# Nearest-neighbour upsampling: 512 consecutive rows per partition, larger DMA descriptors, loads on a second queue

## The chip, the cores and the metric

The kernel runs on one core of a Trainium2 chip. The metric is device time in microseconds (us). A time quoted below is the median of a kernel's runs. "Span" is the length of one profiled execution; it is 1.8 us shorter than the time of that same run (for the kernel before, the record does not say which run was profiled).

## The reference

Every element of a float32 array of shape (16, 64, 64, 64) is repeated twice in both image directions. Nothing is computed.

```python
for i in range(new_h):          # 128
    for j in range(new_w):      # 128
        result[:, :, i, j] = x[:, :, i // 2, j // 2]
```

A core has 16 DMA engines, which move data between HBM (the large memory outside the core) and SBUF (the core's own memory, 128 partitions). A descriptor moves one contiguous run of bytes, and the trace shows it as one packet. The input has 65,536 rows of 64 floats (256 bytes each, 16.8 MB). Each input row becomes two equal output rows of 512 bytes, which lie next to each other in HBM (67.1 MB in all).

## The kernel before

A tile gives each of the 128 partitions K = 32 consecutive input rows. One tile of output is therefore one contiguous stretch of 4 MiB, and neighbouring partitions are 32 KiB apart in it. VectorE expands the first half of the rows, ScalarE the second half: four strided copies each. All loads are issued first, on SyncE's DMA queue, into eight buffers that hold the whole input. The 16 stores follow on the same queue, from two u buffers.

```python
K = 32; rows = P * K; J = 2
# group = 8, which is all of the input
for ti in range(ti0, ti0 + group):
    xt = xpool.tile([P, J, K, W], fdt, name="xt")
    # ... (the first tile comes as two loads of 1 MiB)
    src = src.rearrange("(j p k) w -> p j (k w)", j=J, p=P)   # 8 KiB runs
    nc.sync.dma_start(out=xt[:, :, :, :], in_=src)
for t in range(ti0 * J, (ti0 + group) * J):
    u2 = upool.tile([P, K, s, W, s], fdt, name="u2")          # two buffers
    # ... rows 0..15 on VectorE, 16..31 on ScalarE, for each hd and wd:
    #     copy u2[:, lo:hi, hd, :, wd] <- xt[:, j, lo:hi, :]
    nc.sync.dma_start(out=of[r0 : r0 + rows, :], in_=u2[:, :, :, :, :])  # 32 KiB runs
```

## Time and profile before

| | before |
|---|---|
| time | 200.81 us (200.73 to 201.08, 3 runs) |
| span | 199.2 us |
| VectorE / ScalarE busy | 20% / 34% |
| packets of the 16 DMA engines | 98.5% of the span |
| longest part of the chain | stores, 67% |

These lines are from the page of the kernel before. The rows DMA and GB/s cut the span into 40 slices: the busy share in tenths, and what was moved. The line q1 is the DMA queue table: packets, MB, and the time of its packets as a share of 16 engines' span. The last two lines are the chain of work that ended last, by engine and by line.

```profile
span 199.2 us, 246 instructions
...
DVE 40.0 (20%) x64; ACT 68.0 (34%) x65; POOL 0.2 (0%) x4
...
DMA  6999999999999999999999999999999999999995
GB/s 214 423 438 421 423 421 424 421 500 421 421 421 421 421 421 441 480 447 421 421 421 421 421 421 461 474 428 428 421 421 421 424 421 467 461 421 421 428 428 217
...
q1 hardware_dynamic: 4496, 83.89, 98.5%
...
DMA 69%; ACT 18%; SPq 3%; ACTq 1%; issue 0%
DMA out_dram<-u 67%; ACT u L88 18%; SPq L90 3%; DMA xt<-in_x_dram 2%; ACTq L121 1%; ACTq L88 0%
```

The DMA engines have no hole from the second slice to the second last. The 18% of ScalarE on the chain are not a bottleneck: those copies run while the other u buffer is being stored. The timeline shows it, here at three steady tiles (start, duration, engine, what, and in brackets the idle time before and what ended it).

```profile
101.10 4.18 ACT L88 COPY u<-xt 128x1024 f32<-128x1024 f32 x4 [5.54 <-DMA out_dram<-u]
...
110.80 4.18 ACT L88 COPY u<-xt 128x1024 f32<-128x1024 f32 x4 [5.53 <-DMA out_dram<-u]
...
120.51 4.16 ACT L88 COPY u<-xt 128x1024 f32<-128x1024 f32 x4 [5.52 <-DMA out_dram<-u]
```

One tile takes 9.7 us, of which ScalarE idles 5.5. The trace also records every packet. A 32 KiB store packet takes 1.213 us, nearly without exception, and eight of them on an engine are the 9.7 us of a tile. So the time is the sum of packet times on one engine, plus the start and the tail. Only fewer, shorter or better filled packets can change it.

### The profile page before, as it was taken

What the parts mean: (1) busy time and instruction counts of PE and PEld (TensorE: products, weight loads), DVE (VectorE), ACT (ScalarE), POOL (GpSimd) and SP (SyncE); (2) the same over time, 40 slices, a digit from 0 to 9 for tenths busy, and PEclk for the clock granted to TensorE, in tenths of its full rate; (3) what the DMA queues carried; (4) which work ended last, traced back from release to release, by engine and by line L of the source; (5) the groups of instructions that cost most, each with busy time, mean ns of one, the idle gap of its engine ahead of it and who ended that gap; (6) DMA issues with size and microseconds to landing.
All of it is one profiled execution on the core that took longest, in us unless ns stands there. A gap on an engine that the chain in (4) does not pass through costs nothing.

```text
span 199.2 us, 246 instructions
## 1 busy us (share of the span) xinstructions
DVE 40.0 (20%) x64; ACT 68.0 (34%) x65; POOL 0.2 (0%) x4
## 2 busy tenths in 40 slices
DVE  0810000000404050505050505050505050504000
ACT  2870000000444352626161708080808080808000
POOL 0000000000000000000000000000000000000000
DMA  6999999999999999999999999999999999999995
GB/s 214 423 438 421 423 421 424 421 500 421 421 421 421 421 421 441 480 447 421 421 421 421 421 421 461 474 428 428 421 421 421 424 421 467 461 421 421 428 428 217
DMA packets 4499, 83.90 MB, mean 421 GB/s; under 512 B 401, under 2 KB 401, under 8 KB 401
## 3 DMA queue, kind: packets, MB, share of 16 engines
q1 hardware_dynamic: 4496, 83.89, 98.5%
q14 instruction: 3, 0.02, 0.0%
HBM read 16.78 MB, written 67.11 MB: 421 GB/s over the span
## 4 chain that ended last, share of the span: by engine, by line
DMA 69%; ACT 18%; SPq 3%; ACTq 1%; issue 0%
DMA out_dram<-u 67%; ACT u L88 18%; SPq L90 3%; DMA xt<-in_x_dram 2%; ACTq L121 1%; ACTq L88 0%
## 5 line engine op out<-in xcount | busy, mean ns | idle before, releaser
L88 ACT COPY u<-xt 128x1024 f32<-128x1024 f32 x64 | 66.7, 1136 | 114.6 <-DMA out_dram<-u 111.0
L86 DVE COPY u<-xt 128x1024 f32<-128x1024 f32 x64 | 40.0, 690 | 141.7 <-DMA out_dram<-u 136.1
L88 ACT ACT_TABLE_LOAD x1 | 1.3, 1283 | 0.7 <-PEq L107 0.7
L107 POOL MEMSET const-uint8-127<- 128x1 uint8 x1 | 0.1, 102 | 0.0
L107 POOL MEMSET const-bfloat16-1.0<- 128x1 bf16 x1 | 0.1, 101 | 0.0
L107 POOL MEMSET const-float32-0.0<- 128x1 f32 x1 | 0.1, 99 | 0.2 <-issue 0.2
L107 POOL MEMSET const-float32-1.0<- 128x1 f32 x1 | 0.1, 98 | 0.0
## 6 DMA issues: line engine op xcount, KB each, us to landing
out_dram<-u SPq DMA_DIRECT2D x16, 4096.0 KB, 15.1
xt<-in_x_dram SPq DMA_DIRECT2D x7, 2048.0 KB, 24.4
xt<-in_x_dram SPq DMA_DIRECT2D x2, 1024.0 KB, 5.8
```

The source lines that it names most:

```text
L86: nc.vector.tensor_copy(out=dst, in_=src_ap)
L88: nc.scalar.copy(out=dst, in_=src_ap)
L90: nc.sync.dma_start(out=of[r0 : r0 + rows, :], in_=u2[:, :, :, :, :])
L107: nc = _bacc.Bacc("TRN2", target_bir_lowering=False, num_devices=1)
L121: with _tile.TileContext(nc) as tc:
```

## The change

The intent is larger descriptors. Partition p owns input rows 512p to 512p+511. A load takes 128 of them (32 KiB descriptors where 8 KiB were), a store takes K = 64 (64 KiB where 32 KiB were). Three other things come with it:

- Neighbouring partitions are now 512 KiB apart in the output, and 128 KiB apart in the input.
- Loads are issued by ScalarE, on a second DMA queue. The xt buffers hold half of the input, so two of the four loads are issued between stores.
- VectorE takes 40 of 64 rows.

```diff
-    xf = x.rearrange("b c h w -> (b c h) w")
-    of = out.rearrange("b c (h hd) w -> (b c h) (hd w)", hd=s)
-    K = 32
+    RP = R // P
+    xf = x.rearrange("b c h w -> (b c h) w").rearrange("(p r) w -> p r w", p=P)
+    of = out.rearrange("b c (h hd) w -> (b c h) (hd w)", hd=s).rearrange(
+        "(p r) w -> p r w", p=P
+    )
+    K = 64
     J = 2
+    KV = 40
# ... (xt: 2 buffers of J*K rows; u: 2 buffers)
+    def load(c):
+        xt = xpool.tile([P, J * K, W], fdt, name="xt")
+        nc.scalar.dma_start(
+            out=xt[:, :, :], in_=xf[:, c * J * K : (c + 1) * J * K, :]
+        )
+        xts[c] = xt
+    for c in range(min(2, nloads)):
+        load(c)
+    for t in range(nloads * J):
# ... (copies as before, rows 0..KV on VectorE, KV..K on ScalarE)
-                nc.sync.dma_start(out=of[r0 : r0 + rows, :], in_=u2[:, :, :, :, :])
+        nc.sync.dma_start(
+            out=of[:, t * K : (t + 1) * K, :], in_=u[:, :, :, :, :]
+        )
+        if j == J - 1 and c + 2 < nloads:
+            load(c + 2)
```

More of the change, by code (lines that the diff above doesn't have):

```diff
@@ L14 @@
     x: bass.AP,
-    scale_factor: bass.AP,
+    scale_factor: int,
     out: bass.AP,
@@ L19 @@
     P = nc.NUM_PARTITIONS
-    s = int(scale_factor) if not isinstance(scale_factor, bass.AP) else None
-    assert s is not None and s >= 1
+    s = int(scale_factor)
     B, C, H, W = x.shape
@@ L26 @@
     fdt = x.dtype
-    esz = 4 if fdt == mybir.dt.float32 else mybir.dt.size(fdt)
-    xf = x.rearrange("b c h w -> (b c h) w")
-    of = out.rearrange("b c (h hd) w -> (b c h) (hd w)", hd=s)
-    K = 32
-    while K > 1 and R % (P * K) != 0:
-        K //= 2
-    assert R % (P * K) == 0, f"{R} input rows not tileable into {P} partitions"
-    rows = P * K
-    ntiles = R // rows
-    J = 2
-    while ntiles % J != 0:
-        J //= 2
-    n_in = ntiles // J
-    u2_bytes = K * s * W * s * esz * 2
@@ L44 @@
-    xt_bytes = J * K * W * esz
-    group = max(1, min(n_in, (200 * 1024 - u2_bytes) // xt_bytes))
-    while n_in % group != 0:
-        group -= 1
-    k_dve = (K + 1) // 2
-    with (
-        tc.tile_pool(name="xin", bufs=group) as xpool,
-        tc.tile_pool(name="uexp", bufs=2) as upool,
-    ):
-        for ti0 in range(0, n_in, group):
-            xts = {}
-            for ti in range(ti0, ti0 + group):
-                xt = xpool.tile([P, J, K, W], fdt, name="xt")
-                if ti == 0:
-                    for j in range(J):
-                        nc.sync.dma_start(
-                            out=xt[:, j, :, :],
-                            in_=xf[(ti * J + j) * rows : (ti * J + j + 1) * rows, :],
-                        )
-                else:
-                    src = xf[ti * J * rows : (ti + 1) * J * rows, :]
-                    if J > 1:
-                        src = src.rearrange("(j p k) w -> p j (k w)", j=J, p=P)
-                    nc.sync.dma_start(out=xt[:, :, :, :], in_=src)
-                xts[ti] = xt
-            for t in range(ti0 * J, (ti0 + group) * J):
-                ti, j = divmod(t, J)
-                r0 = t * rows
-                xt = xts[ti]
-                u2 = upool.tile([P, K, s, W, s], fdt, name="u2")
-                for ei, (lo, hi) in enumerate(((0, k_dve), (k_dve, K))):
-                    if lo >= hi:
-                        continue
-                    src_ap = xt[:, j, lo:hi, :]
-                    for hd in range(s):
-                        for wd in range(s):
-                            dst = u2[:, lo:hi, hd, :, wd]
-                            if ei == 0:
-                                nc.vector.tensor_copy(out=dst, in_=src_ap)
-                            else:
-                                nc.scalar.copy(out=dst, in_=src_ap)
-                nc.sync.dma_start(out=of[r0 : r0 + rows, :], in_=u2[:, :, :, :, :])
@@ new lines @@
+    RP = R // P
[4 more added lines that the diff above has]
+    K = 64
+    J = 2
+    nloads = RP // (J * K)
+    assert nloads * J * K == RP
+    KV = 40
+    xpool = ctx.enter_context(tc.tile_pool(name="xin", bufs=2))
+    upool = ctx.enter_context(tc.tile_pool(name="uexp", bufs=2))
+    xts = {}
+    def load(c):
[4 more added lines that the diff above has]
+        xts[c] = xt
@@ new lines @@
+    for c in range(min(2, nloads)):
+        load(c)
+    for t in range(nloads * J):
+        c, j = divmod(t, J)
+        xt = xts[c]
+        u = upool.tile([P, K, s, W, s], fdt, name="u")
+        for lo, hi, copy in ((0, KV, nc.vector.tensor_copy), (KV, K, nc.scalar.copy)):
+            for hd in range(s):
+                for wd in range(s):
+                    copy(
+                        out=u[:, lo:hi, hd, :, wd],
+                        in_=xt[:, j * K + lo : j * K + hi, :],
+                    )
+        nc.sync.dma_start(
+            out=of[:, t * K : (t + 1) * K, :], in_=u[:, :, :, :, :]
+        )
+        if j == J - 1 and c + 2 < nloads:
+            load(c + 2)
```

## The prediction

"The same page" in the text below is "DMA: Bandwidth & Descriptors" of the Trainium skill. Its 214 GB/s, the full rate, was measured at a pitch of 4 MiB padded by 4 KiB.

> **What bounds the kernel now.** The 16 DMA engines. The DMA queue table puts their packets at 98.5% of the 199.2 us span. The slice table shows DMA at 9 in every slice but the first and the last. In the chain of waits, 69% is DMA (67% stores). VectorE (20% busy) and ScalarE (34%) idle mainly for "DMA out_dram<-u" (136 and 111 us). The timeline repeats every 9.71 us, which is exactly eight 32 KiB packets of 1.213 us on each engine.
>
> The packet records add up to it. Each engine moves 128 store packets of 32 KiB, 1.2136 us each: 155.3 us. And 128 load packets of 8 KiB, 0.317 us each: 40.6 us. Together 195.9 us. The remaining 3.3 us are start (first data near 1.7 us) and tail (last packet ends at 198.0 us).
>
> **What the change does.**
> - Load packets go from 8 KiB to 32 KiB. If a 32 KiB read takes what a 32 KiB write takes now, 32 x 1.213 = 38.8 us: saves 1.8 us.
> - Store packets go from 32 to 64 KiB. Fitting the two sizes (0.309 us undisturbed at 8 KiB, 1.213 us at 32 KiB) gives about 8 ns fixed per packet and 27.2 B/ns. So 64 x 2.418 = 154.7 us: saves 0.6 us, or nothing if a 64 KiB run is split in two.
> - Loads move to ScalarE's queue and interleave with the stores, where before all loads came first. I assume that this leaves the total the same.
> - The first load is 4 MiB: it lands near 12.5 us where the first 1 MiB took to 5.5 us. The copies of tile 0 take some 6.5 us, so store 0 issues near 19.5 us. The second load keeps the engines busy until about 22 us: no hole. Afterwards 6.5 us of copies hide behind a 19.4 us store.
> - The VectorE/ScalarE rebalance is off the critical path.
> - If the 1.28 us activation-table load sits before the first load on ScalarE, the start slips by up to 1.3 us.
>
> Balance without any slowdown of the stores: 200.8 - 2.4 + 0 to 1.3 = 198.4 to 199.7 us. All of it is on the critical path, because that is DMA packet time.
>
> **The risk.** Stores now step 512 KiB between partitions (32 KiB before), all engines in step. The same page (Latency and other measured facts, HBM row pitch at large powers of two) gives 207 GB/s per direction at 512 KiB pitch against 214[...], 3% less, for copies between HBM tensors. Here writes run at 432 GB/s, so the effect could be absent or larger. 3% on 155 us is 4.7 us, an estimate from that page: about 203.5 us. I give a visible slowdown of the stores roughly one chance in three.
>
> **Predicted: 200.0 us, 80% range 197.2 to 208.** Faster by over 2%: 0.08; within 2%: 0.62; slower by over 2%: 0.30.
>
> **What would show it.**
> - Right: DMA share still about 98%; 32 KiB reads near 1.21 us; 64 KiB writes near 2.42 us (or 32 KiB pieces at 1.213); no slice below 9 after the first; chain of waits still mainly stores.
> - Pitch at work: store packets longer than 2.42 us, GB/s below 420 in the late slices that hold only stores, while the DMA share stays near 98%.
> - Wrong on overlap: a slice near 20 us, or later, with the DMA share falling, and copies waiting for xt.
>
> **What would make it wrong.** A strong pitch effect on the writes (far over 3%); reads and writes mixed on one engine running better or worse than alone; a hole in the DMA at the first store or at a load that is too late.

## The result, and the profile after

The changed kernel takes 203.61 us (202.75 to 204.12, 4 runs) against 200.86 us of the kernel before beside it. The ratio is 1.0131, 95% interval 1.0102 to 1.016. It is 1.3% slower: inside the 2% that count as the same, but clear of the noise.

These are the same lines of the page of the changed kernel. Queue q1 now carries stores only, and q10 (ScalarE's) the loads.

```profile
span 201.4 us, 147 instructions
...
DVE 45.5 (23%) x32; ACT 50.6 (25%) x33; POOL 0.2 (0%) x4
...
DMA  7999989799999999999998999999999999999990
GB/s 286 443 417 417 521 319 501 312 417 410 527 417 417 430 417 417 443 391 365 430 514 384 430 443 443 456 456 430 417 417 430 417 417 456 430 443 443 469 443 39
...
q1 hardware_dynamic: 1152, 67.11, 77.8%
q10 hardware_dynamic: 576, 16.78, 20.1%
...
DMA 68%; ACT 15%; ACTq 1%; issue 0%
DMA out_dram<-u 62%; ACT u L59 15%; DMA xt<-in_x_dram 6%; ACTq L98 1%; ACTq L59 0%
```

The packets still fill 97.9% of the span (77.8 + 20.1), so the time is still packet time. The last slice has hardly any traffic (39 GB/s where 217 were). The first half has slices on either side of 417 GB/s, while from the 23rd slice to the second last they are about as steady as before. A packet is booked whole where it starts, so single slices swing, in GB/s and in the busy share; read them over several slices. The 8, 7 and 8 in the sixth, eighth and 22nd slice are not holes: worked out from the packets' durations, the engines are busy for all of every stretch of 5 us from 5 to 195 us.

The timeline of the changed kernel shows the start as predicted.

```profile
0.72 0.85 ACTq L45 DMA_DIRECT2D xt<-in_x_dram  x2
1.61 1.28 ACT L59 ACT_TABLE_LOAD   x1 [1.61 <-PEq L84]
12.84 12.18 ACT L59 COPY u<-xt 128x1536 f32<-128x1536 f32 x8 [9.95 <-DMA xt<-in_x_dram]
...
19.03 149.27 SPq L63 DMA_DIRECT2D out_dram<-u  x8
25.05 0.37 ACTq L45 DMA_DIRECT2D xt<-in_x_dram  x1
```

The loads are issued before the table load, so that costs nothing. Load 0 lands near 12.8 us, and the first store issues at 19.0 us, while load 1 still occupies the engines.

The rest is in the packet records. For each packet size the commonest duration is taken as the undisturbed one: 0.309 us for 8 KiB (nearly half of these packets), 0.611 for 16 KiB, 1.213 for 32 KiB, 2.418 for 64 KiB. The sum of these for one engine is called nominal below. What packets took beyond it is called excess (all packets, divided by 16). "Lag" is how much later the last of the 16 engines ends than their mean. This table is worked out from the records, in us.

```
          nominal  excess: start, rest   mean of 16 ends  last end   lag    span
before     194.82        0.58    0.53         197.25       197.96    0.72  199.19
after      193.57        0.64    2.63         198.43       199.98    1.55  201.36
```

("Start" is the first 5 us.) Packet sizes did save 1.25 us. But the excess grew by 2.16 us and the lag by 0.83 us. The span grew by 2.17: -1.25 + 2.16 + 0.83 leaves 0.4 us in short gaps and in the tail, which is not followed further. (The profiled run took 203.14 us; two of the four runs took 204.1 and were not profiled.)

The excess is not spread evenly. From 100 us on, when only stores are left, the mean of the 64 KiB packets is 2.418 to 2.419 us in every stretch of 5 us. Nearly all of it lies in the stretches 20 to 30, 45 to 50, 80 to 85 and 90 to 100 us: there nearly every engine has one or two packets that are about 0.2 to 0.8 us too long, at nearly the same moment. These are times where loads start or end beside the stores.

### The profile page after: what moved, and what is told of

It is laid out like the page before. It is cut to its first block, busy times and chain, and to the rows that moved or that the text cites. A ratio compares the mean times of both kernels' runs of the same rounds, so it can differ in the third digit from the quotient of the medians.

```text
span 201.4 us, 147 instructions
## 1 busy us (share of the span) xinstructions
DVE 45.5 (23%) x32; ACT 50.6 (25%) x33; POOL 0.2 (0%) x4
## 3 DMA queue, kind: packets, MB, share of 16 engines
q1 hardware_dynamic: 1152, 67.11, 77.8%
q10 hardware_dynamic: 576, 16.78, 20.1%
## 4 chain that ended last, share of the span: by engine, by line
DMA 68%; ACT 15%; ACTq 1%; issue 0%
DMA out_dram<-u 62%; ACT u L59 15%; DMA xt<-in_x_dram 6%; ACTq L98 1%; ACTq L59 0%
## 5 line engine op out<-in xcount | busy, mean ns | idle before, releaser
L59 ACT COPY u<-xt 128x1536 f32<-128x1536 f32 x32 | 49.3, 1654 | 115.7 <-DMA out_dram<-u 105.8
L59 DVE COPY u<-xt 128x2560 f32<-128x2560 f32 x32 | 45.5, 1491 | 122.0 <-DMA out_dram<-u 109.1
```

Of the source, the lines that this page charges most:

```text
L59: copy(out=u[:, lo:hi, hd, :, wd], in_=xt[:, j * K + lo : j * K + hi, :],)
```

## The experiments

Two things that the change did at once could be to blame. **Theory A** says that two active queues cost the time. **Theory B** says that the wide pitch of 512 KiB does. A two by two of kernels tells them apart; the changed kernel is one corner.

### Two by two: queue and pitch

Loads on SyncE's queue, behind and before the stores:

```diff
-        nc.scalar.dma_start(
+        nc.sync.dma_start(
```

> The changed kernel with its loads issued from SyncE, so that loads and stores share one DMA queue; addresses and sizes as changed. Theory A (two queues active at once cost time: long packets of 2.5 to 3.2 us where one DMA starts while the other queue is busy, and an engine left one packet behind): about 198.5 us (197.8 to 199.7), store packets 2.418 us throughout, excess over the undisturbed times below 1 us per engine, engines within 1 us of each other at the end. Theory B (the 512 KiB pitch of the stores costs it): no change, 202.7 to 204.2 us.

Measured: 204.73 us, ratio 1.0209. Theory A falls at the wide pitch: with one queue the kernel is slower still. Theory B's "no change" is missed too, by 0.5 us.

Narrow pitch, both queues. A partition owns 128 consecutive rows of one load: descriptors as in the changed kernel, output pitch 128 KiB, input pitch 32 KiB.

```diff
-    ... .rearrange("(p r) w -> p r w", p=P)
+    ... .rearrange("(n p r) w -> n p r w", p=P, r=128)      # xf and of
-            out=xt[:, :, :], in_=xf[:, c * J * K : (c + 1) * J * K, :]
+            out=xt[:, :, :], in_=xf[c, :, :, :]
-            out=of[:, t * K : (t + 1) * K, :], ...
+            out=of[c, :, j * K : (j + 1) * K, :], ...
```

> The changed kernel with a partition owning 128 consecutive rows of a load (output pitch 128 KiB instead of 512, input pitch 32 KiB instead of 128); descriptors and both queues as changed. Theory A (two queues): no change, 202.5 to 204.5 us, with the same long packets where loads and stores overlap. Theory B (pitch): 198 to 199.7 us and no long packets.

Measured: 202.54 us, ratio 1.0098. That is at the lower edge of theory A's range; theory B alone does not hold either.

Both edits together:

> Both undone: pitch 128 KiB and one queue. Theory A: the same as with one queue alone, about 198.5 us. Theory B: the same as with the smaller pitch alone, about 199 us. If both effects are real and add up, this is the fastest of the four and each of the single ones lies between it and 203.6 us.

Measured: 200.30 us (200.18 to 201.02), ratio 0.9981 (0.9969 to 0.9993). The profiled run is the slowest of the six (201.02 us), so this kernel's trace shows 0.7 us more than its median. The four corners (203.61 is from an earlier session, whose kernel before had the same median to 0.1 us):

| time, us | one queue | two queues |
|---|---|---|
| pitch 128 KiB | 200.30 | 202.54 |
| pitch 512 KiB | 204.73 | 203.61 |

With one queue the pitch costs 4.4 us; with two, 1.1 us. At the narrow pitch the second queue costs 2.2 us; at the wide pitch it gains 1.1. The two effects are both real, and they do not add up.

Call each change of the DMA engines from loads to stores, or back, a turn. In the one-queue kernels it is plain where the time goes, because the packets run in the order of the issues: 16 loads, 16 stores, 8 loads, 16 stores, 8 loads and 32 stores on each engine, five turns. The next two answers are the busy times by stretch (columns: stretch, length, busy times of VectorE, ScalarE and GpSimd, clock, DMA share, GB/s). In the stretch 55 to 75 us the engines turn from stores to load 2 and back, in 105 to 125 us to load 3 and back, and from 125 us on nearly everything is a store. First the one-queue kernel with the wide pitch:

```profile
55.00:75.00 20.00, 5.70 (x4) 6.25 (x4) 0.00 (x0) 1.00 0.96 367
...
105.00:125.00 20.00, 5.70 (x4) 6.20 (x4) 0.00 (x0) 1.00 0.96 374
125.00:195.00 70.00, 11.40 (x8) 12.39 (x8) 0.00 (x0) 1.00 1.00 433
```

Then the one-queue kernel with the narrow pitch:

```profile
55.00:75.00 20.00, 5.70 (x4) 6.19 (x4) 0.00 (x0) 1.00 0.99 419
...
105.00:125.00 20.00, 5.71 (x4) 6.20 (x4) 0.00 (x0) 1.00 1.00 433
125.00:195.00 70.00, 11.40 (x8) 12.39 (x8) 0.00 (x0) 1.00 1.00 434
```

In the long stretch the wide pitch costs nothing: 433 against 434 GB/s. In the stretches with a turn it moves 367 and 374 GB/s where the narrow one moves 419 and 433. The engines do not wait for work (the shares from 0.96 to 1.00 come of the booking; by the packets' durations all of these stretches are full): their packets take longer. This is **Theory C**: a wide pitch makes each turn expensive, and a steady stream of stores is not affected.

### Pitch without mixing

The kernel before, with nothing changed but that a partition owns 512 rows; all loads still come first:

```diff
-    xf = x.rearrange("b c h w -> (b c h) w")
+    xf = x.rearrange("b c h w -> (b c h) w").rearrange("(p r) w -> p r w", p=P)
# ... of likewise; loads take xf[:, i*K : ...], stores of[:, t*K : (t+1)*K, :]
```

> The kernel before with one thing changed: a partition owns 512 consecutive rows (stores of 32 KiB at 512 KiB pitch, later loads of 16 KiB descriptors), all loads up front on the same single queue. Theory A: slightly faster than before by the fewer load packets, 199.3 to 200.3 us, store packets still 1.213 us. Theory B: slower than before by 3 to 6 us (204 to 207 us), store packets above 1.23 us.

Measured: 201.18 us, ratio 1.0018 (1.0006 to 1.003). This kernel turns once. Its 32 KiB store packets took 1.213 us on average at 512 KiB pitch, so steady stores are unhurt here too. It saves 0.4 us nominally (194.42) by its 16 KiB loads, but its excess outside the start is 1.40 us where 0.53 were, and 1.2 us of it lie at its one turn, on the last loads. Its loads have larger packets as well as the pitch, so this run does not say which of the two makes that turn dear. Both theories missed it, each on its own side.

### Loads or stores: which pitch matters?

These two kernels give a wrong result: loads and stores no longer agree on which rows a partition owns. One queue in both. The first takes the narrow mapping for the loads only:

```diff
# the one-queue kernel, wide pitch
-    xf = ... .rearrange("(p r) w -> p r w", p=P)
+    xf = ... .rearrange("(n p r) w -> n p r w", p=P, r=128)   # of stays wide
```

> Wrong result on purpose. The one-queue kernel with only the stores at the wide pitch (512 KiB); loads at the narrow one (32 KiB). The first four runs felled theory A: one queue with the wide pitches took 204.7 us, with the narrow ones 200.3, and the long packets sit where the engines turn from loads to stores or back. Theory C (wide store pitch makes each turn dear): about 204.7 us, excess of all packets about 5.3 us per engine. Theory D (wide load pitch): about 200.3 us, excess about 1.5 us. Theory E (both needed, reads and writes colliding): between, or near 200.3 us in both half-wide kernels.

Measured: 204.82 us, ratio 1.0196; result wrong. Excess 5.01 us. By stretch:

```profile
55.00:75.00 20.00, 5.70 (x4) 6.19 (x4) 0.00 (x0) 1.00 1.02 400
...
105.00:125.00 20.00, 5.70 (x4) 6.20 (x4) 0.00 (x0) 1.00 0.97 374
125.00:195.00 70.00, 11.40 (x8) 12.36 (x8) 0.00 (x0) 1.00 1.00 433
```

The second takes the narrow mapping for the stores only:

> Wrong result on purpose. The counterpart: only the loads at the wide pitch (128 KiB), stores at 128 KiB instead of 512. Theory C: about 200.3 us, excess about 1.5 us. Theory D: about 204.7 us, excess about 5.3 us. Theory E: near 200.3 us or between.

Measured: 200.38 us, ratio 0.9975; result wrong. Excess 1.52 us. By stretch:

```profile
55.00:75.00 20.00, 5.70 (x4) 6.18 (x4) 0.00 (x0) 1.00 0.98 419
...
105.00:125.00 20.00, 5.70 (x4) 6.17 (x4) 0.00 (x0) 1.00 0.99 426
125.00:195.00 70.00, 11.40 (x8) 12.34 (x8) 0.00 (x0) 1.00 1.00 434
```

With one queue, the pitch of the stores is responsible, and that of the loads does not matter. Yet most of the long packets of the first of these kernels are loads: of its 5.01 us of excess, 3.61 us are load packets and 1.40 us store packets. Around each of the two later loads, each engine loses on average 0.7 us on the last store packet before them, 0.5 us on the first three load packets, and 0.8 us on the last two, before stores begin again.

The pitch is not parted from two things that go with it: the stretch of output over which one store spreads (16 MiB at 128 KiB, all 64 MiB at 512), and that all pitches tried are powers of two.

### Is it per turn?

Loads of half the size (16 KiB packets where 32 KiB were), one after each store: 9 turns where 5 were.

```diff
-    J = 2
+    J = 1
-    xpool = ... bufs=2
+    xpool = ... bufs=4          # and load(c + 4) after each store
```

> The one-queue kernel with the wide pitches and loads of 2 MiB, one after each store: 9 turns between loads and stores in place of 5. If each turn costs what it did there (excess 4.8 us outside the start over 5 turns, about 0.95 us each), excess rises to about 9 us and the time to 208 to 210 us. If the cost goes with the bytes moved near a turn or with time, not with turns, it stays at 204 to 206 us.

Measured: 209.65 us, ratio 1.0433. The excess outside the start is 9.32 us, which is 1.04 us a turn over nine turns. With five turns it was 4.76 us, or 0.95 us a turn. The first turn differs, as the next section shows; without it (excess from 30 us on) it is 8.30 us over eight turns and 4.13 us over four, 1.04 and 1.03 us a turn. The bytes are the same and the nominal sum is only 0.3 us higher (193.86), so the cost goes with the number of turns.

### How wide is wide?

A partition owns 256 rows of an output stretch (store pitch 256 KiB), one queue, five turns:

```diff
+    ... "(n p r) w -> n p r w", p=P, r=256     # xf and of; indices [c // 2], [t // 4]
```

> Between the one-queue kernels with a store pitch of 512 KiB (204.7 us, 4.8 us of excess outside the start) and of 128 KiB (200.3 us, 0.9 us): store pitch 256 KiB, load pitch 64 KiB, same sizes, same 5 turns. Theory C with a gradual effect: 201.5 to 203.5 us. A threshold would put it at either end.

Measured: 201.34 us, ratio 1.0033; excess outside the start 1.83 us. The time is 0.2 us below the range for a gradual effect, and the excess is not at either end. And 64 rows, so that a store is one contiguous stretch; a load then consists of 16 KiB descriptors:

```diff
+    xf = ... .rearrange("(n j p r) w -> n p j r w", p=P, r=64, j=2)
+    of = ... .rearrange("(n p r) w -> n p r w", p=P, r=64)
```

> The other end: store pitch 64 KiB (a store is one contiguous 8 MiB stretch), loads of 16 KiB descriptors at 16 KiB pitch, same 5 turns, one queue. If the cost of a turn falls on with the pitch: excess outside the start below 0.9 us, 199.5 to 200.3 us although its loads have twice the packets (0.3 us more). If 128 KiB is already free of it: 200.3 to 200.8 us.

Measured: 201.00 us (200.36 to 201.21), ratio 1.0003; excess outside the start 0.87 us, the same as at 128 KiB. Both expectations, 199.5 to 200.3 us and 200.3 to 200.8, were missed. Worked out from the packet records:

| store pitch, one queue, five turns | 64 KiB | 128 KiB | 256 KiB | 512 KiB |
|---|---|---|---|---|
| excess outside the start, us | 0.87 | 0.87 | 1.83 | 4.76 |
| of it at the first turn (5 to 30 us) | 0.81 | 0.33 | 0.78 | 0.63 |
| of it at the four later turns | 0.06 | 0.54 | 1.04 | 4.13 |
| time, us | 201.00 | 200.30 | 201.34 | 204.73 |

The equal totals at 64 and 128 KiB are a coincidence of two parts. The first turn costs 0.3 to 0.8 us and does not follow the pitch: with the narrow stores and wide loads above it cost 0.66 us, with the wide stores and narrow loads 0.30. The four later turns do follow it: 0.02, 0.14, 0.26 and 1.03 us a turn, with the jump between 256 and 512 KiB. Each figure comes from one profile (at 128 KiB from the slow run; the kernel with only the loads wide had 0.06 us a later turn there). Why the first turn is different is not known.

### The second queue

Is it ScalarE's queue, or having two? All DMA on ScalarE, narrow pitch:

```diff
-        nc.sync.dma_start(        # stores
+        nc.scalar.dma_start(
```

> The narrow kernel with loads and stores all issued from ScalarE. If two queues active at once made the two-queue narrow kernel slow (202.5 us, one engine a packet behind): 200.0 to 200.9 us, as with all on SyncE. If ScalarE's queue itself is at fault: 202 us or more.

Measured: 210.37 us, ratio 1.0473. Both expectations missed, because the edit did something else besides. These lines of its timeline show it:

```profile
42.41 1.66 ACT L59 COPY u<-xt 128x1536 f32<-128x1536 f32 x1 [17.10 <-DMA out_dram<-u]
...
42.49 0.35 ACTq L63 DMA_DIRECT2D out_dram<-u  x1
```

Tile 1 had been copied by 25.3 us, but its store is issued only at 42.5 us. The issue stands behind a copy for tile 2 in ScalarE's order, and that copy waits until store 0 has freed its buffer. By then the engines have run dry. They carry packets for 198.7 us of a span of 208.6; in the one-queue kernel on SyncE it was 195.2 of 199.2. The holes thus cost 5.8 us more. The other 3.6 us are excess (5.08 us against 1.48), and that at the narrow pitch: from 30 us on it is 4.21 us, about as much as at 512 KiB. So a wide pitch is not the only thing that makes turns dear, and this run does not answer its question. The packets do in part: in the two-queue kernels the undisturbed loads on ScalarE's queue take 1.213 us, like those on SyncE's, so the queue itself does not move data more slowly.

In the narrow kernel with two queues, ten engines end at 196.8 to 197.2 us and the other six at 198.9 to 199.2. Between the two profiled narrow kernels, two queues have 1.0 us more excess (2.49 against 1.48) and 0.4 us more lag (1.49 against 1.10), which is about the 1.4 us between these two runs; the medians differ by 2.2. At the wide pitch two queues have less excess (3.27 us against 5.27 with one) but more lag (1.55 against 1.02), and this is where the two effects fail to add up.

The last run asks whether this lag is one packet of the other queue: the same kernel with K = 32, J = 4, KV = 20, so stores of 32 KiB packets.

> The narrow two-queue kernel (202.5 us; six of its engines end about 2.1 us after the other ten, nearly one 64 KiB packet) with stores of 32 KiB packets, twice as many (0.6 us more packet time per engine). If the lag is one packet of the other queue, kept because both queues stay fed: engines end about 1.2 us apart in two groups, and the time is 201.5 to 202.2 us. If the lag does not depend on the packet: two groups 2 us apart, 203.0 us or more. If the two queues now leave no groups: about 201 us.

Measured: 201.56 us (200.80 to 201.87, 6 runs), ratio 1.0023; two runs took 200.8, and the profiled one, 201.66, is of the slower four. The two groups are gone; the 16 ends spread from 197.1 to 198.5 us, and the lag is 0.9 us instead of 1.49. The excess fell as well (1.95 against 2.49 us). This agrees with a lag that grows with the packet, but the time is at the edge of one expectation without its two groups, and it does not show the mechanism. A lag as long (1.60 us) stands in the one-queue kernel with nine turns, so it does not take two queues.

### A version to beat both

Narrow pitch, one queue, all four loads first in 32 KiB descriptors, then 16 stores in 32 KiB descriptors (K = 32, J = 4, KV = 20, four xt buffers):

> A version meant to beat both: one queue, narrow pitch (128 KiB out, 32 KiB in), all four loads of 4 MiB in 32 KiB descriptors first, then 16 stores in 32 KiB descriptors: one turn only. Packet sum 38.8 + 155.3 = 194.1 us per engine, plus about 1.1 us of long packets at the start as before and 3.1 us of start and tail: span 198.3, time about 199.5 us, 0.6 % faster than before. Every theory says at least this: faster than the 200.3 us of the one-queue narrow kernel.

Measured: 201.43 us, ratio 1.002: a miss. The nominal sum is 194.08 us, 0.74 us less than before. But its single turn, near 40 us, cost 1.0 us, where the turn of the kernel before, with loads of 8 KiB packets and a store pitch of 32 KiB, cost under 0.1 us. Which difference makes that turn free was not tried; a narrow pitch and a single turn were not enough.

No version with a right result beats the kernel before by more than the 0.2% of the narrow one-queue kernel.

## Why the prediction was right or wrong

It said 200.0 us, within 2% as the likeliest outcome, and a range of 197.2 to 208. The time was 203.61 us, in the range and within 2%. The gain from packet sizes was right in kind. The number was 3.6 us too low, because the balance has no term for what the change costs beside it. That the risk paragraph names "about 203.5 us" is luck: it stood for stores that are slower throughout, and those did not occur.

- **Packet sizes: right in kind, too large.** The 64 KiB packets take 2.418 us, to the digit, and the 32 KiB reads 1.213 us. But "saves 1.8 us" for the loads was mis-sized: the 0.317 us per 8 KiB packet is a mean that contains 1.0 us of excess, half of it at the start, which larger packets do not remove. On undisturbed times the loads save 0.7 us (39.55 against 38.82) and the stores 0.5 us: 1.25 us, not 2.4.
- **Start and overlap: right.** Load 0 landed near 12.8 us (12.5 predicted), store 0 was issued at 19.0 us (19.5), there was no hole at the first store, and the table load cost nothing.
- **The step that failed is "I assume that this leaves the total the same"** for loads interleaved with stores. The excess outside the start is 2.63 us against 0.53, and the lag 1.55 us against 0.72. The prediction named "reads and writes mixed on one engine running better or worse than alone" as what could make it wrong, but gave it no term.
- **The pitch was looked for in the wrong place.** The prediction expected it in "the late slices that hold only stores". There it is absent: 2.418 us a packet. With one queue it acts only around turns (204.73 us wide, 200.30 narrow), and only the store pitch matters. With two queues it is worth 1.1 us, and which pitch does it was not tried.
- **Undoing both** the second queue and the wide pitch returns the 3.3 us (203.61 to 200.30), with the large descriptors kept. That is shown. Undoing one alone gives 202.54 or 204.73 us. Why turns cost more at a wide store pitch is not shown: no run looks into the memory. The run with all DMA on ScalarE had costly turns at the narrow pitch too; its engines came out of each hole within 0.15 us of each other. Being in step does not explain the wide kernel, though: shortly before its stores gave way to loads, its engines were 0.6 and 1.0 us apart, as those of the narrow one-queue kernel were (0.55 and 1.1). The cause stays open.

## What to carry to other kernels

When DMA packets fill the span, work out what a larger descriptor saves from the commonest packet time of each size, not from the mean: 8, 32 and 64 KiB packets here differ by little more than their bytes. Look at what the rearrangement does to the addresses and to the order of loads and stores: a store pitch of 512 KiB was free in a steady stream and cost about 1 us at every turn after the first, where 128 KiB or less cost 0.02 to 0.14 us. So where loads run between stores, try a narrow store pitch, and compare the late and the mixed stretches of the profile separately. Neither a narrow pitch nor a single turn is a guarantee: the version with all loads first lost 1.0 us at its only turn, and the one with holes paid about 1 us a turn, both at 128 KiB.

## What the Trainium skill lacked or had wrong

- "DMA: Bandwidth & Descriptors", Latency and other measured facts (HBM row pitch at large powers of two) gives 207 GB/s per direction at 512 KiB pitch against 214 at a padded pitch (4 MiB and 4 KiB), for copies between HBM tensors. Here steady stores from SBUF at 512 KiB pitch lose nothing (433 GB/s against 434 at 128 KiB). The loss comes at turns between loads and stores: about 1.03 us each after the first at 512 KiB, 0.26 at 256, 0.14 at 128 and 0.02 at 64. Those copies read and write throughout, so the two observations may have one cause; no run here shows that.
- The same page, Issuing engines are not separate DMA queues, says that issuing from several engines only saves the sequencer's time. Here it was not neutral: 202.54 us with loads on a second queue against 200.30 on one (pitch 128 KiB), and 203.61 against 204.73 at 512 KiB. (With two queues the loads also overlap the stores, where on one they take turns; the two are not parted here.) Nor does the page say how far apart the 16 engines can end: 2.4 us between the first and the last with two queues and large packets, but 2.5 us also with one queue and nine turns.
- No page that was read gives the cost of a turn between loads and stores on one queue: from under 0.1 us (the kernel before) to 1.2 us (the same kernel at 512 KiB pitch).
